# Elementwise work of the key stage moved from POOL to VectorE and ScalarE, and triangular inverses taken three batches at a time

## The chip, the cores and the metric

One NeuronCore of one Trainium2 chip. The metric is the device time of one execution in microseconds; lower is better. The engines are named as in the profile: PE (TensorE; PEld its weight loads), DVE (VectorE), ACT (ScalarE), POOL (GpSimd), SP (SyncE, whose queue issues most transfers). In the kernel's code they are T, V, S, G and SP.

## What is computed

Two layers on 512 tokens of width 1024 (with 256 context tokens ahead of them in layer 0): an RWKV-7 mixer with inner width 2048, 32 heads of 64 and two directions, then a Hyena mixer (a long convolution). All in fp32. The change lies in layer 0, whose heart is this recurrence, run forwards (z = 0) and backwards (z = 1):

```
def step(s, inp):
    r_t, w_t, k_t, v_t, a_t, b_t = inp
    sa = jnp.einsum('bhvk,bhk->bhv', s, a_t)
    s = s * w_t[:, :, None, :] + sa[..., None] * b_t[:, :, None, :] + v_t[..., None] * k_t[:, :, None, :]
    return s, jnp.einsum('bhvk,bhk->bhv', s, r_t)
```

with a = -kk, b = kk * a_gate, kk the normalised key, w the decay, and k scaled by the gate. Beside it stands a bonus, the sum over a head of r * (k_0 + k_1) * r_k, times v, where k_0 and k_1 are the keys of the two directions.

## The kernel before

**Tiling.** The inner width is 16 pairs p of two heads (128 partitions). The 768 positions are 12 chunks of 64. Inside a chunk the recurrence becomes matrix products: with e the running product of decays, the scaled vectors ar (from kk and r, times e) and bk (from kk * a and k, divided by e) give a strictly triangular 64x64 matrix L for each head, chunk and direction, and the chunk needs the inverse of (I - L). Each L is taken as two 32x32 diagonal blocks, inverted by elimination, and one off-diagonal block that is put in later.

**Stages.** (1) Norms, mixes and the product for v. (2) The key stage: products for k and r run on PE; `k_out`, `k_norm` (normalise), `decays` (decay and gate from small products, tanh, and a running sum along each chunk: the scan instruction), `key_side` (exponentials, bk, ar, gam) and `strict_side` (L by PE, stored to DRAM as ld; ar, bk, gam stored too) work through the 16 pairs and both directions; `bonus` follows each pair. (3) The scan stage: `merge` completes the inverses of a pair (its transfers are issued by POOL, MQ = G.dma_start), `fetch` and `prep` load and prepare chunks, and `chain` runs the recurrence for two pairs at a time, in 8 rounds of 12 steps; products for the gate (g), read-out and output product run beside it. (4) Filters and layer 1, untouched by the change. In the profiled execution the key stage's pairs run from about 300 to 775 us and the chain from 884 to 1697 us.

**The inverses** (`inverse`, lines 1228 to 1245). The 384 units of a direction (16 pairs x 2 heads x 12 chunks) are cut into 6 batches of 64. A batch is a tile lt of 128 partitions (64 units x 2 diagonal blocks) by 32x32, loaded from ld by two SP transfers. For j = 1 to 30 DVE multiplies a column by a row into ltm, j x (31-j) elements, and adds that to lt: 60 dependent instructions. POOL then clears the other triangle (affine_select) and sets the diagonal, and SP stores the batch to td. With two directions there are 12 batches; IB = 2 of a direction's 6 belong to the key stage, the others to the scan stage. A batch may start when both directions have stored enough pairs (`ready_inv`, line 1252); `merge` of a pair waits for its batches.

**Who runs what.** Tuples such as E_KE name the engines an operation may use (lines 1033 to 1038): E_CU scales the decay argument, E_TA the gate ta, E_KE and E_ET are the two products k * em and em * ta, E_AR and E_RC the two halves of ar. In `bonus` and for gam the engine is fixed.

**The order of the work** is not written out by hand. `run` (line 255) holds a set of lanes, each a generator that yields operations, and places one operation after another by a list schedule: of all next operations the one that the cost model (`Model.price`, line 183) lets start first. Where an operation may go to several engines, the price is added to the start and the smaller sum wins. The model prices DVE at 0.064 us + n/960 (n/1920 for one input in SBUF), ACT at 0.1 + n/1200 and more for tensor scale and bias. Each engine then executes its own list in order. The key stage ends when all its lanes (`key_lanes`, line 1257, the inverses of IB among them) are done, the products of g apart; only then the lanes of the scan stage are added.

**A step of the chain** (lines 1498 to 1551): products into PSUM, copied to xs by ACT and DVE; a product with the inverse, copied into sv by ACT and DVE; a product giving bs; DVE adds the carried state (sa = bs + sc); DVE multiplies sa by the decay gam into the next step's sv, one half of the partitions at a time; POOL forms the next sc = sa * gam. sa has one buffer, sc two.

## Time and profile before

| | us |
|---|---|
| median of 3 runs | 2401.1 (2401.01 to 2407.73) |
| the profiled execution | 2397.8 |
| its span, first to last instruction | 2396.1 |

| engine | busy us, share of the span |
|---|---|
| PE | 2054.1, 86% |
| PEld (weight loads, beside PE) | 1625.3, 68% |
| DVE | 1776.7, 74% |
| ACT | 1067.5, 45% |
| POOL | 650.5, 27% |

The time that counts is that of the whole execution; the span leaves out what lies before the first and after the last instruction. Busy time is the union of an engine's instructions. All instructions go through one helper line (58), so the profile is read by the names of tiles: `out<-in`. Shapes are partitions x elements.

### The profile page before, as it was taken

To read this page: it belongs to the slowest core of one execution; us is meant where nothing else is said; L and a number is where in the kernel's file an instruction comes from. 1 tells how busy PE (TensorE), PEld (TensorE's weight loads), DVE (VectorE), ACT (ScalarE), POOL (GpSimd) and SP (SyncE) were. 2 spreads that over 40 slices of the span, in tenths; PEclk is the share of its full clock that TensorE was granted. 3 is DMA by queue.
4 is the path that set the end of the run, shared out by engine and by line. 5 is a ranking of instruction groups with operands and counts; after the bars stand their busy time and mean duration, and the time that the engine had idled before them with its cause. 6 is when DMAs were issued, how large, how long until landed. Compare 5 with 4: busy or idle time off the path is not lost.

```text
span 2396.1 us, 53878 instructions
## 1 busy us (share of the span) xinstructions
PE 2054.1 (86%) x21710; PEld 1625.3 (68%) x21710; DVE 1776.7 (74%) x2971; ACT 1067.5 (45%) x1891; POOL 650.5 (27%) x745
## 2 busy tenths in 40 slices
PE   6699888779787688778888788898769999999997
PEld 2588666567665567666666667676447787878786
DVE  1955399999997677777888787767677675757666
ACT  2534576657664234333445344434444333333333
POOL 0400174655564422233233233321132100000000
PEclk8799999989988898888999999999989999999999
DMA  7155666747467675646585754554456523223232
GB/s 235 47 182 196 210 203 191 227 161 239 167 199 240 179 187 142 155 121 145 152 187 135 160 144 127 144 125 133 128 178 206 179 79 105 84 89 103 82 121 78
DMA packets 317568, 369.29 MB, mean 154 GB/s; under 512 B 132387, under 2 KB 203630, under 8 KB 317320
## 3 DMA queue, kind: packets, MB, share of 16 engines
q1 hardware_dynamic: 303832, 330.34, 47.0%
q0 software_dynamic: 13488, 35.52, 5.1%
q8 instruction: 171, 2.80, 0.5%
q14 instruction: 77, 0.63, 0.1%
HBM read 262.79 MB, written 102.17 MB: 152 GB/s over the span
## 4 chain that ended last, share of the span: by engine, by line
PE 38%; DVE 18%; DMA 8%; issue 5%; SPq 3%; ACT 2%; POOL 2%; DVEq 0%; ACTq 0%; POOLq 0%
PE ps L58 38%; DVE sv L58 3%; SPq L58 3%; DVE ltm L58 2%; DVE lt L58 2%; DVE wlo L58 2%; DVE ar L58 2%; DMA tt<-td 1%; DMA lt<-ld 1%; DMA ar<-ard 1%; DVE cvv L58 1%; DVE sa L58 1%; DMA ar<-zd 1%; POOL tt L58 1%; DVE xs L58 1%
## 5 line engine op out<-in xcount | busy, mean ns | idle before, releaser
L58 PE MATMUL ps<-m,whi 128*128 128x512 f32 (+1 forms) x1536 | 419.9, 375 | 45.2 <-DVE ro L58 15.8
L58 DVE TENSOR_TENSOR wlo<-wraw,whi 128x512 fp32r<-128x512 f32 x320 | 245.9, 770 | 209.0 <-ACT whi L58 206.0
L58 ACT ACTIVATE whi<-wraw 128x512 fp32r<-128x512 f32 x320 | 200.9, 628 | 411.8 <-PE ps L58 321.9
L58 PEld LDWEIGHTS ps<-m,whi 128*128 128x128 f32 x1536 | 263.3, 197 | 102.2 <-DVE ro L58 17.0
L58 PE MATMUL ps<-ar,bk 128*64 128x64 f32 (+2 forms) x4096 | 224.7, 249 | 53.4 <-DVE ar L58 40.7
L58 PE MATMUL ps<-m,wlo 128*128 128x512 f32 (+1 forms) x768 | 245.9, 371 | 0.0
L58 PEld LDWEIGHTS ps<-ar,bk 128*64 128x64 f32 (+1 forms) x4096 | 193.5, 147 | 75.7 <-issue 42.9
L58 PE MATMUL ps<-h1h,whi 128*128 128x512 f32 x512 | 201.1, 393 | 1.7 <-DVE cx L58 1.1
L58 PE MATMUL ps<-h1l,whi 128*128 128x512 f32 x512 | 199.9, 390 | 0.4 <-DVE h1l L58 0.4
L58 PE MATMUL ps<-h1h,wlo 128*128 128x512 f32 x512 | 199.8, 390 | 0.0
L58 POOL TENSOR_TENSOR sc<-sa,gam 128x256 f32<-128x256 f32 x80 | 66.4, 831 | 449.1 <-DVE sa L58 439.9
L58 DVE TENSOR_TENSOR ltm<-lt 128x30 f32<-128x30 f32 (+4 forms) x360 | 154.2, 428 | 25.2 <-DMA lt<-ld 13.6
L58 DVE TENSOR_TENSOR lt<-lt,ltm 128x30 f32<-128x30 f32 (+4 forms) x360 | 149.7, 416 | 9.6
L58 PEld LDWEIGHTS ps<-m,wlo 128*128 128x128 f32 x768 | 133.9, 197 | 25.9 <-issue 2.8
L58 POOL TENSOR_TENSOR res<-res,gt 128x512 f32<-128x512 f32 x4 | 5.4, 1372 | 498.6 <-ACT junk L58 498.6
L58 DVE TENSOR_TENSOR ar<-ps,cst 64x512 f32<-64x512 f32 (+1 forms) x192 | 115.0, 599 | 16.7 <-PE ps L58 11.3
L58 PE MATMUL ps<-sv,bt 128*64 128x64 f32 x1408 | 92.0, 242 | 26.2 <-DVE sv L58 13.8
L58 PEld LDWEIGHTS ps<-h1h,whi 128*128 128x128 f32 x512 | 96.2, 188 | 21.3 <-issue 1.5
L58 PEld LDWEIGHTS ps<-h1l,whi 128*128 128x128 f32 x512 | 96.2, 188 | 20.4 <-DVE h1l L58 1.5
L58 PEld LDWEIGHTS ps<-h1h,wlo 128*128 128x128 f32 x512 | 96.1, 188 | 19.6
L58 PE MATMUL ps<-sv,ar 128*64 128x64 f32 x1536 | 89.0, 238 | 20.9 <-DVE sv L58 19.2
L58 PEld LDWEIGHTS ps<-sv,bt 128*64 128x64 f32 x1408 | 70.1, 148 | 53.5 <-DVE sv L58 19.8
(292 smaller groups left out, 4739.9 us busy)
## 6 DMA issues: line engine op xcount, KB each, us to landing
wraw<-wg SPq DMA_DIRECT2D x128, 256.0 KB
wraw<-w SPq DMA_DIRECT2D x128, 256.0 KB
aw<-ada_w SPq DMA_DIRECT2D x96, 256.0 KB
bkd<-bk SPq DMA_DIRECT2D x32, 768.0 KB
ard<-ar SPq DMA_DIRECT2D x32, 640.0 KB
ar<-ard SPq DMA_DIRECT2D x128, 128.0 KB
ar<-zd SPq DMA_DIRECT2D x128, 128.0 KB
wraw<-w_out SPq DMA_DIRECT2D x64, 256.0 KB
```

Source lines behind the costliest of these rows:

```text
L58: return getattr(self.eng.eng, self.fn)(*self.a, **self.k)
```

## The change

- The tuples lose G: E_CU and E_TA become (S, V); E_KE, E_ET and E_RC become (V,); the two POOL operations of the bonus go to DVE and the copy of gam to ACT.
- `inverse` handles NI = 3 batches in one tile, [128, 3, 32, 32], with the same 60 instructions, each three times as long. Six loads come ahead, three stores behind. IB = 1 triple of a direction (of 2) belongs to the key stage, and `ready_inv` asks for three batches' worth of pairs, that is 192 units, 8 pairs.
- In the chain sa is no longer a tile: the sum is made in sc, and POOL multiplies sc in place. sc has one buffer.
- l21 in `merge` loses its direction axis (the directions lie in different partitions), and the space reserved for the descriptors of POOL's transfers is halved.

```diff
@@ -536,6 +536,7 @@
     ard = [[tl(dr, f"ard{p}_{z}", [P, NC + NCX, C]) for z in range(2)] for p in range(NP)]
     NU = NP * 2 * NC
     UB = 64
+    NI = 3
     NB = NU // UB
     ld = [tl(dr, f"ld{z}", [C, NU, C]) for z in range(2)]
     td = [[tl(dr, f"td{z}_{b}", [2, UB, 32, 32]) for b in range(NB)] for z in range(2)]
@@ -1030,12 +1031,12 @@
     AB = 1
     MB2 = 0.0
     KN = 1
-    E_CU = (S,G)
-    E_TA = (S,G)
-    E_KE = (G,V)
-    E_ET = (V,G)
+    E_CU = (S,V)
+    E_TA = (S,V)
+    E_KE = (V,)
+    E_ET = (V,)
     E_AR = (V,)
-    E_RC = (G,)
+    E_RC = (V,)
     lring, gamring, bkring = Ring(LB), Ring(2), Ring(BS)
     taring, curing, arring = ([Ring(n) for _ in range(2)] for n in (DT, DC, AB))
     ktile, pair, uses = {}, {}, {}
@@ -1147,7 +1148,7 @@
         bb, em = bk[:, :, 0], bk[:, :, 1]
         yield S.activation(out=em, in_=cu[:, :, tok], func=AF.Exp, scale=-1.0)
         yield S.activation(out=cu, in_=cu, func=AF.Exp)
-        yield G.tensor_copy(out=gam[:, :, z:z + 1], in_=cu[:, :, last:last + 1])
+        yield copy(S, gam[:, :, z:z + 1], cu[:, :, last:last + 1])
         while p not in ktile:
             yield
         k, nk = ktile[p]
@@ -1211,9 +1212,9 @@
             yield
         ts = [gset[p, z][0][:, NCC:] for z in range(2)]
         q = ts[0]
-        yield G.tensor_tensor(out=q, in0=q, in1=ts[1], op=ADD)
+        yield V.tensor_tensor(out=q, in0=q, in1=ts[1], op=ADD)
         used(p, ("ta", 1), 2, gset[p, 1][1])
-        yield G.tensor_tensor(out=q, in0=q, in1=k[:, NCC:], op=MUL)
+        yield V.tensor_tensor(out=q, in0=q, in1=k[:, NCC:], op=MUL)
         used(p, "k", 3, ktok[p])
         yield V.scalar_tensor_tensor(out=q, in0=q, scalar=pcol("r_k", p), in1=r, op0=MUL, op1=MUL)
         used(p, "r", 3, rt_)
@@ -1227,30 +1228,34 @@
 
     def inverse(z, bt):
 
-        lt = tl(sysp[0], "lt", [P, 32, 32], sysp[1])
-        u0 = bt * UB
-        for bl in range(2):
-            q = slice(32 * bl, 32 * bl + 32)
-            yield dma(out=lt[HR[bl]], in_=ld[z][q, u0:u0 + UB, q].rearrange("s u t -> u s t"))
-        v = lt[:, ::-1, ::-1] if z else lt
-        tmp = tl(sysp[0], "ltm", [P, 240], sysp[2])
+        lt = tl(sysp[0], "lt", [P, NI, 32, 32], sysp[1])
+        for k in range(NI):
+            u0 = (bt * NI + k) * UB
+            for bl in range(2):
+                q = slice(32 * bl, 32 * bl + 32)
+                yield dma(out=lt[HR[bl], k], in_=ld[z][q, u0:u0 + UB, q].rearrange("s u t -> u s t"))
+        v = lt[:, :, ::-1, ::-1] if z else lt
+        tmp = tl(sysp[0], "ltm", [P, NI * 240], sysp[2])
         for j in range(1, 31):
             w = 31 - j
-            tv = tmp[:, 0:j * w].rearrange("p (a b) -> p a b", b=w)
-            yield V.tensor_tensor(out=tv, in0=v[:, 0:j, j:j + 1].broadcast_to([P, j, w]), in1=v[:, j:j + 1, j + 1:32].broadcast_to([P, j, w]), op=MUL)
-            yield V.tensor_tensor(out=v[:, 0:j, j + 1:32], in0=v[:, 0:j, j + 1:32], in1=tv, op=ADD)
-        yield G.affine_select(out=lt, in_=lt, pattern=[[2 * z - 1, 32], [1 - 2 * z, 32]], compare_op=ALU.is_gt, fill=0.0, base=0, channel_multiplier=0)
-        yield G.memset(lt.rearrange("p a b -> p (a b)")[:, ::33], 1.0)
-        yield dma(out=td[z][bt].rearrange("b u s t -> (b u) s t"), in_=lt)
-        invdone.add((z, bt))
-
-    IB = 2
+            tv = tmp[:, 0:NI * j * w].rearrange("p (k a b) -> p k a b", k=NI, b=w)
+            yield V.tensor_tensor(out=tv, in0=v[:, :, 0:j, j:j + 1].broadcast_to([P, NI, j, w]),
+                                  in1=v[:, :, j:j + 1, j + 1:32].broadcast_to([P, NI, j, w]), op=MUL)
+            yield V.tensor_tensor(out=v[:, :, 0:j, j + 1:32], in0=v[:, :, 0:j, j + 1:32], in1=tv, op=ADD)
+        yield G.affine_select(out=lt, in_=lt, pattern=[[0, NI], [2 * z - 1, 32], [1 - 2 * z, 32]], compare_op=ALU.is_gt, fill=0.0, base=0,
+                              channel_multiplier=0)
+        yield G.memset(lt.rearrange("p k a b -> p k (a b)")[:, :, ::33], 1.0)
+        for k in range(NI):
+            yield dma(out=td[z][bt * NI + k].rearrange("b u s t -> (b u) s t"), in_=lt[:, k])
+            invdone.add((z, bt * NI + k))
+
+    IB = 1
     invdone = set()
     keys = [Lane([(decays, p, z) for p in range(NP)]) for z in range(2)]
     bons, norms = Lane(), Lane()
 
     def ready_inv(_, b):
-        return min(ldone) * 2 * NC >= (b + 1) * UB
+        return min(ldone) * 2 * NC >= (b + 1) * NI * UB
     invs = Lane([(inverse, z, b) for b in range(IB) for z in range(2)], 1, lambda z, b: ready_inv(z, b))
     mods1 = Lane([(adaln, ((0, 2), (1, 0), (1, 1), (1, 2)), adp, 128, 4, 1, (adp, "arow"))], 1, lambda *a: True, MB2)
     rlane2 = Lane([(rate_loads, p) for p in range(NP)])
@@ -1320,14 +1325,14 @@
     def merge(p):
 
         tt = tts[p % len(tts)]
-        l21 = rt("l21", [P, 2, NC, 32], LBUF)
+        l21 = rt("l21", [P, NC, 32], LBUF)
         t1 = rt("t1", [P, 2, NC, 32], 1)
         for z in range(2):
             f = slice(32 * z, 32 * z + 32)
             g = slice(32 - 32 * z, 64 - 32 * z)
             for h in range(2):
                 u = (p * 2 + h) * NC
-                yield MQ(out=l21[64 * h + 32 * z:64 * h + 32 * z + 32, z], in_=ld[z][f, u:u + NC, g])
+                yield MQ(out=l21[64 * h + 32 * z:64 * h + 32 * z + 32], in_=ld[z][f, u:u + NC, g])
                 for bl in range(2):
                     rr = slice(64 * h + 32 * bl, 64 * h + 32 * bl + 32)
                     cs = slice(32 * bl, 32 * bl + 32)
@@ -1346,7 +1351,7 @@
         for c in range(NC):
             for z in range(2):
                 for f, g in rows[z]:
-                    yield T.matmul(b[g, c, :], lhsT=l21[f, z, c, :], rhs=t1[f, z, c, :], start=True, stop=True)
+                    yield T.matmul(b[g, c, :], lhsT=l21[f, c, :], rhs=t1[f, z, c, :], start=True, stop=True)
         m1 = tl(rx, "m1", [P, NC, 32], 1, tag="t1")
         yield copy((S, V), m1, b)
         t[0] = True
@@ -1493,7 +1498,7 @@
         sv, stok = svs.pop(0)
         for h in range(2):
             yield G.memset(sv[h][HR[h]], 0.0)
-        sc = rt("sc", [P, 2, 2, C], 2)
+        sc = rt("sc", [P, 2, 2, C])
         yield G.memset(sc, 0.0)
         for n in range(NC):
             g, i = divmod(n, 4)
@@ -1528,17 +1533,15 @@
                 bs = quad("pn")
                 for q, z, h in QZH:
                     yield T.matmul(bs[HR[h], q, z, :], lhsT=BT[q][z][:, lc[z], HR[h]], rhs=sv[h][:, q, z, :], start=True, stop=True)
-                sa = rt("sa", [P, 2, 2, C])
-                yield V.tensor_tensor(out=sa, in0=bs, in1=sc, op=ADD)
+                yield V.tensor_tensor(out=sc, in0=bs, in1=sc, op=ADD)
                 while not svs:
                     yield
                 nsv, ntok = svs.pop(0)
                 gv = gf[:, :, two(2 * (base[0] + lc[0]), 2 * (base[1] + lc[1]) + 1)].unsqueeze(3).broadcast_to([P, 2, 2, C])
                 for h in range(2):
-                    yield V.tensor_tensor(out=nsv[h][HR[h]], in0=sa[HR[h]], in1=gv[HR[h]], op=MUL)
+                    yield V.tensor_tensor(out=nsv[h][HR[h]], in0=sc[HR[h]], in1=gv[HR[h]], op=MUL)
                 if n < NC - 2:
-                    sc = rt("sc", [P, 2, 2, C], 2)
-                    yield G.tensor_tensor(out=sc, in0=sa, in1=gv, op=MUL)
+                    yield G.tensor_tensor(out=sc, in0=sc, in1=gv, op=MUL)
             if g:
                 for q, z, h in QZH:
                     yield T.matmul(by[HR[h], q, z, :], lhsT=sv[h][:, q, z, :], rhs=ARB[q][:, h, z, lc[z], :], start=False, stop=q + z == 2)
@@ -1663,7 +1666,7 @@
     W_PREP = 2
     W_YS = 1
     ys, reads = Lane(width=W_YS, bias=B_YS), Lane([(filter_base,)], bias=B_READ)
-    invs = Lane([(inverse, z, b) for b in range(IB, NB) for z in range(2)], 1, lambda *a: True, B_INV)
+    invs = Lane([(inverse, z, b) for b in range(IB, NB // NI) for z in range(2)], 1, lambda *a: True, B_INV)
 
     def ready_merge(p):
         return zeroed and all((z, b) in invdone for z in range(2) for b in range(-(-(p + 1) * 2 * NC // UB))) \
@@ -2071,7 +2074,7 @@
     import concourse.bacc as _bacc
     from concourse.bass_utils import run_bass_kernel_spmd as _run
 
-    nc = _bacc.Bacc("TRN2", target_bir_lowering=False, num_devices=1, dynamic_dma_scratch_size=8192)
+    nc = _bacc.Bacc("TRN2", target_bir_lowering=False, num_devices=1, dynamic_dma_scratch_size=4096)
     arrays = layout(inputs)
     I = {n: nc.dram_tensor(n, v.shape, mybir.dt.from_np(v.dtype), kind="ExternalInput").ap() for n, v in arrays.items()}
     out = nc.dram_tensor("out", (TX, D), F32, kind="ExternalOutput").ap()
```

## Rows read from the trace of the kernel before

**Rows 1.** The four stages: busy us of each engine (instructions), TensorE clock, DMA share, GB/s
```profile
300.00:775.00 475.00, 387.15 (x3165) 297.65 (x3163) 443.63 (x522) 308.31 (x506) 284.12 (x217) 0.93 0.63 202
775.00:884.00 109.00, 79.94 (x964) 62.50 (x964) 67.28 (x160) 32.78 (x55) 40.82 (x65) 0.89 0.76 199
884.00:1425.00 541.00, 453.79 (x8781) 363.13 (x8782) 435.76 (x970) 220.02 (x457) 155.92 (x242) 0.91 0.60 146
1425.00:1697.00 272.00, 238.78 (x4523) 188.76 (x4520) 194.29 (x350) 117.47 (x232) 71.69 (x112) 0.96 0.50 129
```

**Rows 2.** Key stage, DVE: groups by shape | busy us, mean ns | idle before
```profile
L58 DVE TENSOR_TENSOR wlo<-wraw,whi 128x512 fp32r<-128x512 f32 x59 | 62.6, 1063 | 11.9 <-ACT whi L58 11.8
L58 DVE TENSOR_TENSOR_SCAN cu<-scanm,cu 128x780 f32<-128x780 f32 x28 | 56.2, 2009 | 0.0
L58 DVE TENSOR_TENSOR ar<-nk,cu 128x768 f32<-128x768 f32 x32 | 42.8, 1339 | 0.0
L58 DVE SCALAR_TENSOR_TENSOR bk<-nk,bk 128x768 f32<-128x768 f32 x30 | 33.5, 1119 | 2.5 <-ACT bk L58 2.5
...
L58 DVE TENSOR_TENSOR l2l<-l,l2h 128x512 fp32r<-128x512 f32 x13 | 13.7, 1050 | 0.0
```

**Rows 3.** The same work by tile, whole run: ns least/median/most, first and last start
```profile
L58 DVE TENSOR_TENSOR wlo<-wraw,whi x59: 659/692/2335, 312.0 to 774.1; 128x512 fp32r<-128x512 f32 x59
L58 DVE TENSOR_TENSOR_SCAN cu<-scanm,cu x32: 1751/1776/3445, 273.9 to 745.7; 128x780 f32<-128x780 f32 x32
L58 DVE TENSOR_TENSOR ar<-nk,cu x32: 930/953/2568, 301.2 to 760.4; 128x768 f32<-128x768 f32 x32
```

**Rows 4.** Key stage, POOL: groups | busy us, mean ns
```profile
L58 POOL TENSOR_TENSOR ar<-r,cu 128x512 f32<-128x512 f32 x32 | 49.2, 1539 | 0.1
L58 POOL TENSOR_TENSOR bk<-kk,bk 128x768 f32<-128x768 f32 x21 | 47.0, 2243 | 0.0
L58 POOL TENSOR_SCALAR ta<-ta,kah,ka 128x768 f32<-128x768 f32 x24 | 45.1, 1881 | 49.3 <-DVE bk L58 45.1 <-DMA wraw<-wg 3.0 <-DMA bod<-ta 1.2
L58 POOL TENSOR_SCALAR cu<-cu,cc 128x768 f32<-128x768 f32 x13 | 19.4, 1489 | 4.8 <-ACT cu L58 4.7
```

**Rows 5.** The triangular inverses: busy us (instructions) of DVE, ACT, POOL before and in the scan
```profile
300.00:775.00 475.00, 142.02 (x240) 0.00 (x0) 7.75 (x8) 0.93 0.63 202
775.00:1425.00 650.00, 161.82 (x480) 0.00 (x0) 11.64 (x16) 0.90 0.63 155
```

**Rows 6.** Scan stage, DVE: the inverses' largest and smallest shape | busy us, mean ns
```profile
L58 DVE TENSOR_TENSOR lt<-lt,ltm 128x240 f32<-128x240 f32 x16 | 6.5, 406 | 0.4
L58 DVE TENSOR_TENSOR lt<-lt,ltm 128x30 f32<-128x30 f32 x16 | 3.1, 196 | 0.5
```

**Rows 7.** One-input work on DVE, tile nn: ns least/median/most
```profile
L58 DVE TENSOR_SCALAR nn<-hd x3: 411/418/419, 821.1 to 905.2; 64x512 f32<-64x512 f32 x3
```

**Rows 8.** SP's loads for the inverses by tile: ns least/median/most to issue one
```profile
L58 SPq DMA_DIRECT2D lt<-ld x24: 579/1354/3408, 366.3 to 1326.4; - x24
```

**Rows 9.** Scan stage, DVE: the chain's groups | busy us, mean ns
```profile
L58 DVE TENSOR_TENSOR sv<-sa,gam 64x256 f32<-64x256 f32 x110 | 61.9, 562 | 3.4
L58 DVE TENSOR_TENSOR sa<-ps,sc 128x256 f32<-128x256 f32 x55 | 23.3, 424 | 12.5 <-PE ps L58 10.5
```

**Rows 10.** One step of the chain, instructions in order of time: start us, us
```profile
1005.18 0.42 DVE L58 TENSOR_TENSOR sa<-ps,sc 128x256 f32<-128x256 f32 x1
1005.64 1.18 DVE L58 TENSOR_TENSOR sv<-sa,gam 64x256 f32<-64x256 f32 x2
1005.69 0.86 POOL L58 TENSOR_TENSOR sc<-sa,gam 128x256 f32<-128x256 f32 x1 [6.68 <-DVE sa L58]
```

**Rows 11.** The same multiplications by tile: ns least/median/most
```profile
L58 DVE TENSOR_TENSOR sv<-sa,gam x176: 405/420/858, 884.2 to 1697.7; 64x256 f32<-64x256 f32 x176
```

**Rows 12.** Waits in 884 to 1425 us: total us, times, longest
```profile
PE ps L58 <- DVE sv L58: 26.2, 43, 5.2
```

**Rows 13.** POOL's transfers for the merges by tile: ns least/median/most to issue one
```profile
L58 POOL DMA_DIRECT2D tt<-td x144: 560/615/694, 796.9 to 1558.9; - x144
```

## The prediction

> **What bounds the kernel now.** I read first the busy time of each engine by stage [rows 1]. In the key stage (300 to 775 us) DVE is busy 443.6 of 475 us, 93.4%, and PE 387.2, 81.5%: DVE sets the pace and PE idles 88 us behind it. In the scan stage no engine is full. While inverses run beside the chain (884 to 1425) PE is busy 84% and DVE 81%; afterwards (1425 to 1697) PE 88% and DVE 71%, with the granted clock up from 0.91 to 0.96. So the change is worth what it takes from DVE in the first stage, and what PE waits for DVE in the second.
>
> Then I read the key stage's DVE groups [rows 2] against the medians of the same instructions [rows 3]. The mean is far above the median everywhere: 1063 against 692 ns, 2009 against 1776, 1339 against 953. The same shape sometimes takes over twice its normal time, and POOL, busy 284 us [rows 1], works on the same tiles meanwhile [rows 4]. I take the excess as the price of the two running together.
>
> **The change, key stage.** *Excess returned.* Mean less median times count: wlo 59 x 0.371 = 21.9 us; cu 28 x 0.233 = 6.5; ar 32 x 0.386 = 12.4. Seven further groups, the first and last of which stand in the rows [rows 2], lose 37.2 the same way (0.953 us taken for 768 elements, 0.692 for 512). Together 78.0 us.
>
> *Inverses.* Before, 240 instructions (four batches) take 142.0 us here, while 480 (eight batches) take 161.8 later [rows 5]: 592 against 337 ns each. One instruction handles 165 elements on average (the sum of j(31-j) over 30). Between 30 and 240 elements the time goes from 196 to 406 ns [rows 6], 1.00 ns an element and 166 ns fixed. Three batches in one, 496 elements, give 0.66 us by that line; the nearest row, 512 elements at 692 ns [rows 3], gives 0.675, which I take. A triple is 60 x 0.675 = 40.5 us against 3 x 60 x 0.337 = 60.7. Two triples in this stage: 81.0 instead of 142.0, with six batches done instead of four. The Trainium skill (Perfetto Trace Analysis, Optimizing Scalar/DVE Operations) puts the overhead of a DVE instruction on SBUF at about 60 ns. By it the 480 instructions that go away would save only 29 us; by the 166 ns of the rows it is 80, and the measurement decides.
>
> *Work returned to DVE.* The 42 products on bk (21 of them in [rows 4], 21 more of the same shape) at 0.953: 40.0 us. The 32 products ar<-r,cu and 32 of the bonus at 0.692: 44.3. POOL's 24 + 13 scalings of ta and cu [rows 4] now choose between ACT and DVE. DVE's one-input work took 418 ns for 512 elements [rows 7], so 0.55 to 0.63 for 768. None on DVE gives 0, all 60 of the stage 38; the planner prices DVE at half of ACT, so I take 40 of them, 22 us. The small copies of gam go to ACT: 30, at most at ACT's mean of 0.61 us (308.3 / 506 [rows 1]), 18 us on an engine busy 65%, so nothing; without that cover each would hold up the bk products behind it.
>
> DVE in the stage: 443.6 - 78.0 - 142.0 + 81.0 + 40.0 + 44.3 + 22.0 = 411 us (389 to 427 by the ends). At the same 93.4% that is 440 us, a **gain of 35**, if the load is even. It is not: a triple needs the first eight of the sixteen pairs, so the inverses fall into the second half. First half: DVE 165, PE 387.2 / 2 = 193.6, which now bounds: 207 us at 93.4%. Second half: DVE 246, so 263. Together 471, a gain of 4. If PE holds only the 88% of 1425 to 1697, the first half is 220 and the stage loses 8. I take **15**, between the even and the uneven case, for pairs can run ahead only a little (three k buffers), with -8 and 35 as ends.
>
> *Transfers and queues.* The loads and stores of the inverses are as many as before (24 and 12), but six loads now go to SP in a row: 6 x 1.35 us [rows 8], 8 us in which weight loads stand behind them, four times. Two weight buffers are loaded ahead, so I count nothing; uncovered it is 32 us over the whole run. POOL's clearing of the other triangle becomes three times longer, about 6 us a triple (7.75 / 4 x 3, [rows 5]), but nothing waits for it until a merge. The transition (775 to 884) I leave alone.
>
> **The change, scan stage.** It is 96 steps in eight rounds; 55 of the sums stand in the first stretch [rows 9], 11 a round, so it holds 60 steps and the second 36. PE idle per step is (541 - 453.8) / 60 = 1.45 us against (272 - 238.8) / 36 = 0.92. The excess, 0.53 x 60 = 32 us, goes with the inverses; their DVE time falls from 161.8 to 81, so half of it goes: **16** (0 to 32).
>
> The step: POOL starts sc right after sa, beside the two sv products [rows 10], and these take 1.18 us together where two medians make 0.84 [rows 11]; the mean of 562 ns [rows 9] says that it is so in most steps. In place, sc has to wait until both products have read it. The chain gains 0.34 us in 80 steps, 27 us; PE's wait for sv is 26.2 in the first stretch [rows 12], but that counts both kinds of sv. I take **12** (0 to 26). The new wait holds POOL about 0.8 us longer, with copies of sv and merge transfers queued behind it; POOL had stood idle for 6.68 us before [rows 10], and the next sum needs sc a step later. What is late next is ACT's half of the copies and PE itself.
>
> Clock: at 0.96 instead of 0.91, 453.8 us would be 24 less; with half of the waits gone I take **10** (0 to 24).
>
> Sum: 15 + 16 + 12 + 10 = **53 us**. The profiled execution took 2397.8 (span 2396.1), so 2344.8; the median of the runs is 3.3 higher, so 2348.
>
> The smaller l21 and the dropped copy of sa cost nothing. The halved descriptor space is the slower rival's.
>
> **Rivals.** *Late inverses.* The two triples form one dependent line of 120 instructions, 81 us. If they lose against the key work they run at the stage's end: PE-bound pairs 387 / 0.934 = 414, plus 81, is 495, a loss of 20, against the scan's 38: 2383. For it: readiness comes only at the middle, and DVE is then 94% asked for. Against: before, batches of the same priority ended at their time.
>
> *No difference.* PE takes over as the bound at 88% (the key stage loses 8) and the scan is held by PE's order, so that only one of its three terms comes: within 7 us of 2401.
>
> *The slower side: POOL's transfers.* The space for POOL's descriptors is halved. Now one transfer takes 615 ns to issue and never over 694 [rows 13], so nothing stalls. There are 144 of these and 64 more for l21, 13 a merge. If a full ring made each as long again, POOL would lose 8 us a merge, 128 in all; sc and the sv copies stand behind them. Above 53 / 16 = 3.3 us a merge that reaches the chain the change loses; at half the price and more, 64, it gives 2412. Against: POOL is idle 71% of the scan, and merges run ahead.
>
> *DVE stays saturated.* If the excess is not POOL's doing, 106 us come back to the engine that bounds the stage. The point is 53 x 0.934 = 50 us of the 139 lost (78 and, for the inverses, 142.0 - 240 x 0.337 = 61) staying; with 100 staying it is 2348 + 107 = 2455. The Trainium skill (same page and section) says that work may well be moved off a saturated DVE, even to GpSimd, but adds that the two share a port, so that moving between them might not help; by its first half the change would lose. The trace bears out the second half, for DVE's products grow most while POOL runs beside them [rows 10].
>
> **Chances.** Forecast 0.60; late inverses 0.19; no difference 0.08; POOL's transfers 0.08; DVE saturated 0.05. About 0.3% (7 us) is what a measurement of this kernel can tell from no change. Faster 0.79, same 0.08, slower 0.13. The ends of the terms reach from -8 to 117 us of gain; 2300 to 2402 holds the forecast but for its best corner (0.04), the late inverses and most of no difference, and leaves out the slower cases. The likeliest case alone: 2305 to 2375.
>
> **What would show it.** Right: wlo near 0.70 and ar near 0.95 us in the key stage; 240 inverse instructions in all, of 0.66 to 0.69 us; DVE near 410 us there; the two sv products 0.84 us together; idle of PE per step near 1.2 in the first rounds. Wrong: means that stay above 0.85 for wlo, inverses that end after the last pair's ld, POOL transfers above 0.7 us, or PE busy under 85% in a shorter key stage.

## The result, and the profile after

The changed kernel takes **2301.66 us** (median of 4 runs, 2296.43 to 2309.6) against 2402.41 (2401.01 to 2407.73): a ratio of 0.958, interval 0.9548 to 0.9611, 100.7 us faster. The forecast was 2348, the range 2300 to 2402. The profiled execution of after took 2309.6 us (span 2307.7), the slowest of its four, so the two profiles are 88.2 us apart, not 100.7.

The stages of the changed kernel, which answer to [rows 1], are the key stage, the transition, the first five rounds of the chain and the last three. Each line has the stretch, then the busy us of PE, PEld, DVE, ACT and POOL (with instructions), the granted TensorE clock, the DMA share and GB/s:

```profile
300.00:735.00 435.00, 395.41 (x3257) 301.03 (x3257) 398.62 (x530) 327.71 (x559) 11.29 (x38) 0.95 0.74 232
735.00:860.00 125.00, 94.02 (x1039) 71.74 (x1039) 86.64 (x142) 36.20 (x62) 50.46 (x67) 0.88 0.83 196
860.00:1347.00 487.00, 414.40 (x8710) 333.90 (x8706) 344.01 (x653) 196.67 (x403) 156.72 (x260) 0.93 0.63 152
1347.00:1601.00 254.00, 230.01 (x4454) 183.88 (x4452) 186.86 (x350) 110.96 (x217) 67.01 (x114) 0.97 0.49 130
```

POOL fell from 284.12 to 11.29 us in the key stage and the stage is 40 us shorter, with as much PE work in it. Three dates, counted from the span's start, divide the gain: the last store of ld, the chain's first sum and its last. The first two lines are before, the other two after:

```profile
L58 SPq DMA_DIRECT2D ld<-cu x64: 445/486/1527, 306.0 to 772.7; - x64
L58 DVE TENSOR_TENSOR sa<-ps,sc x88: 403/425/427, 883.8 to 1696.8; 128x256 f32<-128x256 f32 x88
L58 SPq DMA_DIRECT2D ld<-cu x64: 451/487/1530, 311.3 to 731.2; - x64
L58 DVE TENSOR_TENSOR sc<-ps,sc x88: 406/424/427, 859.7 to 1600.6; 128x256 f32<-128x256 f32 x88
```

Up to the last ld it is -41.5, in the transition +17.4 (128.5 instead of 111.1), in the chain -72.1 (740.9 instead of 813.0), and behind it +7.8 (707.1 instead of 699.3): together -88.4 of the span. Three later runs have the changed kernel's plan unaltered (the last three rows of the table below). Their chains take 738.0 to 740.8 us, but their last ld comes at 720.2 to 728.2, so the key stage's gain is 41 to 53 us, and the profile shown here has the least of it.

The groups of DVE in the key stage, beside [rows 2] and [rows 3] (busy us, mean ns | idle before):

```profile
L58 DVE TENSOR_TENSOR_SCAN cu<-scanm,cu 128x780 f32<-128x780 f32 x28 | 49.4, 1773 | 0.7 <-issue 0.7
L58 DVE TENSOR_TENSOR wlo<-wraw,whi 128x512 fp32r<-128x512 f32 x63 | 43.1, 684 | 13.9 <-ACT whi L58 13.1 <-PE ps L58 0.6
...
L58 DVE TENSOR_TENSOR ar<-nk,cu 128x768 f32<-128x768 f32 x32 | 30.4, 949 | 0.5 <-DMA ard<-ar 0.4
...
L58 DVE TENSOR_SCALAR ta<-ta,kah,ka 128x768 f32<-128x768 f32 x15 | 10.1, 674 | 0.1
...
L58 DVE TENSOR_SCALAR cu<-cu,cc 128x768 f32<-128x768 f32 x9 | 5.6, 617 | 3.6 <-ACT cu L58 3.4
```

These three means are now just below what the medians were [rows 3]: 684 ns where the mean was 1063, 949 for 1339, 1773 for 2009. Their whole excess is gone.

The inverses follow: busy us (instructions) of DVE, ACT and POOL in key stage, transition and scan, then by tile (ns least/median/most, first and last start). Their counterpart is [rows 5]:

```profile
300.00:735.00 435.00, 76.83 (x111) 0.00 (x0) 3.74 (x2) 0.95 0.74 232
735.00:860.00 125.00, 44.57 (x70) 0.00 (x0) 8.18 (x4) 0.88 0.83 196
860.00:1601.00 741.00, 41.87 (x60) 0.00 (x0) 3.73 (x2) 0.94 0.58 144
```

```profile
L58 SPq DMA_DIRECT2D lt<-ld x24: 585/1685/4632, 485.4 to 865.1; - x24
L58 POOL TENSOR_SCALAR_AFFINE_SELECT lt<-lt x4: 3462/3624/3840, 613.2 to 974.7; 128x3072 f32<-128x3072 f32 x4
```

All 12 batches take 163.3 us (303.8 before). POOL's clearing, which ends a triple's work, starts at 613.2 for the first and at 974.7 for the last of the four; the other two are at 739.9 and 840.0, so the second triple of the key stage ends 9 us behind the last ld.

Two steps of the chain's own work, beside [rows 10] and [rows 11]:

```profile
1007.01 0.42 DVE L58 TENSOR_TENSOR sc<-ps,sc 128x256 f32<-128x256 f32 x1 [0.76 <-PE ps L58]
1007.47 0.87 DVE L58 TENSOR_TENSOR sv<-sc,gam 64x256 f32<-64x256 f32 x2
...
1008.49 0.62 POOL L58 TENSOR_TENSOR sc<-sc,gam 128x256 f32<-128x256 f32 x1 [5.00 <-DVE sv L58]
```

The two sv products take 0.87 us together, where they took 1.18, and POOL's product starts when they are done and takes 0.62 instead of 0.86. What PE waits for sv over the whole chain (total us, times, longest), before and after, in answer to [rows 12]:

```profile
PE ps L58 <- DVE sv L58: 33.1, 61, 5.2
PE ps L58 <- DVE sv L58: 9.3, 20, 1.0
```

### The profile page after: what moved, and what is told of

It is laid out like the page before. It is cut to its first block, busy times and chain, and to the rows that moved or that the text cites. A ratio compares the mean times of both kernels' runs of the same rounds, so it can differ in the third digit from the quotient of the medians.

```text
span 2307.7 us, 53374 instructions
## 1 busy us (share of the span) xinstructions
PE 2032.2 (88%) x21710; PEld 1606.1 (70%) x21710; DVE 1650.6 (72%) x2646; ACT 1058.7 (46%) x1881; POOL 375.8 (16%) x583
## 4 chain that ended last, share of the span: by engine, by line
PE 52%; DVE 19%; DMA 12%; issue 5%; ACT 3%; SPq 2%; POOL 1%; DVEq 0%; ACTq 0%; POOLq 0%
PE ps L58 52%; SPq L58 2%; DVE wlo L58 2%; DVE bk L58 2%; DVE ar L58 2%; DMA aw<-ada_w 2%; DMA ar<-zd 2%; DMA wraw<-wg 2%; DVE ltm L58 1%; DVE ta L58 1%; DVE sv L58 1%; DVE lt L58 1%; DMA ar<-ard 1%; DVE cvv L58 1%; DMA tt<-td 1%
## 5 line engine op out<-in xcount | busy, mean ns | idle before, releaser
L58 DVE TENSOR_TENSOR wlo<-wraw,whi 128x512 fp32r<-128x512 f32 x320 | 225.8, 707 | 200.8 <-ACT whi L58 198.6
L58 PEld LDWEIGHTS ps<-ar,bk 128*64 128x64 f32 (+1 forms) x4096 | 186.7, 141 | 54.4 <-issue 22.0
L58 POOL TENSOR_TENSOR sc<-sc,gam 128x256 f32<-128x256 f32 x80 | 55.5, 694 | 421.6 <-DVE sv L58 413.5
L58 DVE TENSOR_TENSOR ltm<-lt 128x90 f32<-128x90 f32 (+14 forms) x120 | 81.1, 676 | 20.8 <-DMA lt<-ld 17.5
L58 PE MATMUL ps<-xs,tt 128*64 128x64 f32 x1536 | 68.5, 233 | 28.6 <-DVE xs L58 26.7
L58 POOL DMA_DIRECT2D tt<-td x144 | 87.1, 609 | 9.9 <-DMA zd<-tt 4.9
```

What stands on the lines that cost most here:

```text
L58: return getattr(self.eng.eng, self.fn)(*self.a, **self.k)
```

## The experiments

Every ratio is to the kernel before on the same chip. The dates and the chain's length come from the two rows shown above, of each kernel; g is the PE time that products of g take inside the chain, overlaps counted once.

| kernel | last ld | chain starts | chain, us | g, us | ratio |
|---|---|---|---|---|---|
| before | 772.7 | 883.8 | 813.0 | 24.0 | 1 |
| only POOL emptied | 761.5 | 875.8 | 781.0 | 10.8 | 0.9921 |
| only the sum in place | 775.2 | 885.0 | 780.1 | 24.3 | 0.9876 |
| both, single batches | 762.0 | 876.5 | 761.8 | 10.8 | 0.9816 |
| triples, POOL at work | 788.1 | 913.1 | 751.6 | 5.7 | 0.9919 |
| changed | 731.2 | 859.7 | 740.9 | 0 | 0.958 |
| half of the single batches early | 766.4 | 911.4 | 781.1 | 0 | 1.0037 |
| the same, later | 726.4 | 917.3 | 741.7 | 0 | 0.9851 |
| second triples soft | 721.6 | 847.0 | 776.0 | 0 | 0.9691 |
| second triples held | 728.3 | 844.4 | 778.3 | 0 | 0.9762 |
| no POOL beside the chain | 732.0 | 852.3 | 766.9 | 5.7 | 0.9708 |
| changed, smaller ring still | 728.2 | 857.7 | 740.8 | 0 | 0.9622 |
| changed, g held back | 720.2 | 847.1 | 738.0 | 0 | 0.9583 |
| changed, bias of 0.06 | 724.7 | 850.4 | 738.0 | 0 | 0.962 |

### One part at a time

**Only POOL emptied**: the kernel before with the engines of the key stage changed, and nothing else.

```diff
-    E_CU = (S,G)
+    E_CU = (S,V)
...
-    E_RC = (G,)
+    E_RC = (V,)
...
-        yield G.tensor_tensor(out=q, in0=q, in1=ts[1], op=ADD)
+        yield V.tensor_tensor(out=q, in0=q, in1=ts[1], op=ADD)
```

> The kernel before with only the key stage's elementwise work taken from POOL. If POOL caused the excess: means of wlo and ar at 0.69 and 0.95, inverse instructions at 0.34 instead of 0.59 us, DVE in the stage near 405 us instead of 444, the stage 35 to 45 us shorter, median 2355 to 2370. If the triples brought the key stage's gain: within 10 us of 2402, or slower, as 100 us come to a saturated DVE.

Measured: 2376.43 us, ratio 0.9921 (0.9886 to 0.9955), 19 us faster. Its key stage and its inverses there:

```profile
300.00:766.00 466.00, 401.50 (x3320) 305.90 (x3318) 398.86 (x660) 331.74 (x565) 13.97 (x44) 0.93 0.68 219
```

```profile
300.00:766.00 466.00, 79.11 (x240) 0.00 (x0) 6.69 (x8) 0.93 0.68 219
```

DVE has taken over most of POOL's work (the copies of gam and some of the scalings go to ACT) and is busy 45 us less than before (443.6). The 240 single inverse instructions take 79.1 us (330 ns each) where they took 142.0 [rows 5]: their excess, too, was POOL's. The durations are as expected, but the time is not: the last ld comes only 11 us sooner, where a stage shorter by 35 to 45 was expected. With DVE and PE each busy 86% of it, neither fills the stage. The chain is 32 us shorter, and 13 of that come back behind it (711.9 us instead of 699.3).

**Only the sum in place**: the kernel before without sa.

```diff
-                sa = rt("sa", [P, 2, 2, C])
-                yield V.tensor_tensor(out=sa, in0=bs, in1=sc, op=ADD)
+                yield V.tensor_tensor(out=sc, in0=bs, in1=sc, op=ADD)
...
-                    yield G.tensor_tensor(out=sc, in0=sa, in1=gv, op=MUL)
+                    yield G.tensor_tensor(out=sc, in0=sc, in1=gv, op=MUL)
```

> The kernel before with only the sum of the chain made in sc and multiplied there by POOL. If the step of the chain sets the pace: the two sv products at 0.84 instead of 1.18 us, 0.34 us a step in 80 steps, median 2375 to 2392. If PE's order sets it: products shorter all the same, median within 7 us of 2402.

Measured: 2368.3 us, 0.9876 (0.9832 to 0.9919), 27 us faster, 7 better than expected. All of it lies in the chain, which is 33 us shorter; 8 come back behind it (707.6 us), as in the changed kernel.

**Both, single batches**: the changed kernel with one batch to a tile.

```diff
-    NI = 3
+    NI = 1
...
-    IB = 1
+    IB = 2
```

> The changed kernel with inverses one batch at a time and two of six batches of a direction in the key stage, as before; all else as changed. If the inverses' DVE time counts, the scan stage gets eight batches of 20.2 us (162) instead of six at 13.5 (81): 16 to 32 us more in the first rounds, the key stage unchanged (81 us of inverses either way), median 2318 to 2335. If only POOL's absence counts, 2295 to 2310.

Measured: 2350.17 us, 0.9816 (0.9776 to 0.9856), 45 us faster: the sum of the two above (19 and 27), and slower than either expected range. What remains to the changed kernel, whose four measurements give 0.958 to 0.9622, is 46 to 57 us. It belongs to the triples, their later start and the two more batches of the key stage together.

**Triples, POOL at work**: the changed kernel with the key stage's work back on POOL.

```diff
-    E_CU = (S,V)
+    E_CU = (S,G)
...
-    E_RC = (V,)
+    E_RC = (G,)
...
-        yield V.tensor_tensor(out=q, in0=q, in1=ts[1], op=ADD)
+        yield G.tensor_tensor(out=q, in0=q, in1=ts[1], op=ADD)
```

> The changed kernel with the key stage's elementwise work back on POOL (engine tuples, bonus, copy of gam as before); triples, sum in sc and the rest stay. If the excess on DVE is POOL's doing, the means of wlo and ar in the key stage rise from 0.68 and 0.95 to about 1.05 and 1.3 us, DVE there does some 100 us less own work but pays 80 to 130 us of excess, the stage grows by 20 to 40 us, and the median is 2320 to 2345. If the excess has another cause, the means stay, DVE is freed of 100 us in a stage that it bounds, and the median falls to 2260 or below.

Measured: 2376.64 us, 0.9919 (0.9891 to 0.9948). Its key stage, its inverses in it, and wlo:

```profile
300.00:792.00 492.00, 408.58 (x3237) 311.70 (x3236) 444.82 (x425) 309.11 (x505) 293.63 (x203) 0.92 0.66 207
```

```profile
300.00:792.00 492.00, 112.37 (x120) 0.00 (x0) 8.80 (x4) 0.92 0.66 207
```

```profile
L58 DVE TENSOR_TENSOR wlo<-wraw,whi 128x512 fp32r<-128x512 f32 x64 | 65.6, 1029 | 15.0 <-ACT whi L58 14.9
```

The excess is back (1029 ns), and a triple's instruction takes 936 ns (112.37 / 120) against 692 (76.83 / 111). The last ld is 57 us later than in the changed kernel, and the time lies 32 us above the expected range. Against only the sum in place the triples have won nothing: it is 8 us slower, and the two intervals overlap. **The triples are worth some 50 us with POOL quiet and nothing with POOL at work**; the quiet POOL is worth 19 us without them.

### When the inverses run

**Half of the single batches early, and the same later.** Both have single batches and six of twelve in the key stage, as the changed kernel has in triples. In the first a batch starts as soon as its pairs are stored (after 3, 6 and 8 pairs); the second keeps all of them until 8 pairs are.

```diff
-    NI = 3
+    NI = 1
...
-    IB = 1
+    IB = 3
...
-        return min(ldone) * 2 * NC >= (b + 1) * NI * UB
+        return min(ldone) * 2 * NC >= 3 * UB
```

(The last two lines are in the second alone.)

> The changed kernel with inverses one batch at a time, three of six batches of a direction in the key stage, each ready as soon as its pairs are stored (3, 6 and 8). Against the run with late single batches it differs in timing alone. If timing counts, PE drops to some 38 of 50 us from 400 us on and the ratio is 0.01 or more above that run's. If grouping counts alone, both ratios agree within 0.004.

> The changed kernel with inverses one batch at a time, three of six batches of a direction in the key stage, and none of them ready before eight pairs are stored: the same six batches at the same time as the triples, in 360 instructions instead of 120. If it is the timing that lets PE run freely in the first half, PE is busy 48 of 50 us until about 500 us as with the triples, and the ratio to before is 0.955 to 0.968. If it is the grouping, the second half pays 121 us of inverses instead of 81 and more gaps: chain start 25 to 50 us later than with the triples, ratio 0.973 to 0.99.

Measured: 2403.82 us, 1.0037 (1.0017 to 1.0057), for the first; 2358.74, 0.9851 (0.9827 to 0.9874), for the second. The 50 us from 400 on, the first kernel, the second, and the changed one:

```profile
400.00:450.00 50.00, 39.00 (x307) 29.84 (x306) 43.66 (x80) 33.26 (x57) 1.71 (x5) 0.86 0.57 179
```

```profile
400.00:450.00 50.00, 48.50 (x414) 36.82 (x412) 49.52 (x66) 42.07 (x72) 0.48 (x4) 1.00 0.71 239
```

```profile
400.00:450.00 50.00, 48.54 (x414) 36.82 (x412) 49.51 (x66) 42.03 (x72) 0.49 (x4) 1.00 0.73 238
```

Without inverses in the way PE is busy 97% at the full clock (granted 1.00, the upper of its two levels, 2.4 GHz); with early ones it is 39 us of 50 at 0.86, though DVE is not full. The kernel with only POOL emptied, whose single batches start early too, shows the same in these 50 us: 38.78 at 0.86. The later start lets the pairs end 40 us sooner, so **with POOL quiet it is the late start, and not the grouping, that shortens the key stage**. But 360 single instructions then don't fit behind the key work. From the last ld to the chain the second kernel shows:

```profile
730.00:917.00 187.00, 132.36 (x1228) 95.86 (x1228) 132.19 (x357) 38.63 (x74) 35.29 (x53) 0.75 0.59 152
```

90.4 us of the 132.2 are inverses, and the clock falls to 0.75. This is the rival of late inverses, and the triples, a third as many dependent instructions, are what keeps it away. The first kernel's expectation on timing holds: its ratio is 0.022 above that of both, single batches (0.9816). Of the second kernel's two expectations each holds in one half: PE is busy as timing alone would have it, and the ratio is that of grouping, with the chain 58 us later instead of 25 to 50. Why early batches hold the pairs up by so much, the runs do not settle: PE's waits there end with ar on DVE (23.7 us between 350 and 740), but the second kernel, with DVE fuller, has 5.0 us of them.

**Second triples held, and soft.** Pairs 8 to 15 need the second two triples only in round 4. The first kernel holds them until four pairs are merged; in the second they only give way (a larger bias in the planner).

```diff
-    invs = Lane([(inverse, z, b) for b in range(IB, NB // NI) for z in range(2)], 1, lambda *a: True, B_INV)
+    invs = Lane([(inverse, z, b) for b in range(IB, NB // NI) for z in range(2)], 1, lambda *a: len(mrgd) >= 4, B_INV)
```

```diff
-    B_INV = 0.05
+    B_INV = 1.0
```

> The changed kernel with the second two triples held back until four pairs are merged, since only rounds 4 to 7 need them. Theory: the chain's start at 860 is bound by the work on the way to the first merges, and the 44.6 us that DVE spends on the second triples from 735 to 860 stand in its way; without them the chain starts 5 to 20 us earlier, and in the scan the triples cost about 5 us a pair of them, so 0 to 15 us faster than the changed kernel. Rival: the first triples themselves (the second of them ends at 740) and the merge transfers set the start, so it stays within 4 us of 860, and the scan gets longer by 5 to 10 us.

> The changed kernel with the planner's bias for the second two triples at 1.0 us instead of 0.05, so that they give way to other work but are not held back. Between the changed kernel (chain 860 to 1601, 45 us of the second triples on DVE ahead of the chain and 42 in the scan) and the kernel with them held until four merges (chain 844 to 1623, 86 us of inverses in the scan, 37 us longer chain). Theory: an instruction of 0.7 us in the scan stands in the way of the chain's short ones on DVE, so what counts is how much of the inverses lies in the scan: the chain gets about 0.85 us longer for each us of inverse more in the scan, and starts at most 16 us earlier; with 10 to 30 us moved it comes out 0 to 15 us slower than the changed kernel. Rival: it was the hold itself that cost, since the merges of pairs 8 and on came late (one gap of 34 us between two steps); then the softer bias keeps the earlier start without the late merges, and it is 5 to 15 us faster.

Measured: 2339.47 us, 0.9762 (0.9739 to 0.9785), held; 2322.7, 0.9691 (0.9661 to 0.9721), soft. The chain starts 13 to 15 us sooner than in the profile of the changed kernel, but the last three rows of the table, with that kernel's plan, start it at 847.1 to 857.7. So the date alone shows nothing. From the last ld to the chain the changed plan takes 125.7 to 129.5 us, soft 125.4 and held 116.1: holding the triples back brings 10 to 13 us there, and the softer bias none. The chain is 35 to 37 us longer in both, against a scatter of 3 in the changed plan. The loss lies in its first four rounds: 427.3 us (soft) and 433.4 (held) from the first sum to that of the fifth round, against 391.6. It does not go by the inverses that moved: 13 us of them with soft, 44 with held (55.0 and 86.0 us in the chain against 41.9). Neither theory holds as put: soft has a late gap of 41.1 us between two sums at 1233, where the transfers of the next merges are only being issued, but also gaps of 33 and 28 us earlier, and the changed kernel's longest is 22.6.

### The other suspects

**A smaller ring still.** The changed kernel with half of the descriptor space again.

```diff
-dynamic_dma_scratch_size=4096
+dynamic_dma_scratch_size=2048
```

> The changed kernel with the space for POOL's descriptors halved once more, 2048 for 4096. If a full ring holds POOL back, issues of the merge transfers grow from 0.61 to 0.9 us and more, and the ratio is above 0.965. If the ring never fills, 0.61 us and 0.955 to 0.961 as in the changed kernel.

Measured: 2303.06 us, 0.9622 (0.9599 to 0.9645), the changed kernel's time. Its transfers for the merges come first, then those of the changed kernel:

```profile
L58 POOL DMA_DIRECT2D tt<-td x144: 562/617/654, 765.2 to 1463.4; - x144
```

```profile
L58 POOL DMA_DIRECT2D tt<-td x144: 560/615/652, 768.6 to 1466.2; - x144
```

No issue is longer than it was before [rows 13]: the slower rival's price is nil here.

**No POOL beside the chain**: an attempt to beat the changed kernel by taking the rest of POOL's elementwise work outside the chain as well.

```diff
-    E_SB = (V, G)
+    E_SB = (V,)
...
-    E_FL = (G,V)
+    E_FL = (V,)
...
-    E_GT = (G,V)
+    E_GT = (V,)
...
-    E_FH = (G,)
+    E_FH = (V,)
```

> The changed kernel with the other elementwise work that POOL shares with DVE also given to DVE: shifts in the first stage, the low parts of the filters, the two products with the residual gates (layer 0's rows and the last rows). Excess on DVE beside them should go (the rows' product of 1024 elements at 1.1 instead of up to 5.1 us, the last rows 1 to 3 us earlier): ratio 0.950 to 0.957. If DVE has no room there or the excess is not POOL's: 0.958 or more.

Measured: 2323.86 us, 0.9708 (0.9685 to 0.9731): slower than the changed kernel by 20 us or more. It gains some at the ends (the key stage's first ld comes at 299.2 against 305.9 to 312.6 in the four profiles of the changed plan, what follows the chain is 3.5 us shorter), and the chain, whose code is untouched, gets 26 us longer; 5.7 of them are g's. What the other 20 are, the runs do not show.

**Products of g held back, and a bias of 0.06.** One was to bring the four last g products back into the chain, the other to see what a change of plan without a change of work does.

```diff
+                while g == 3 and p >= 12 and not scanning:
+                    yield
                 while bring.full():
...
+    scanning = []
...
+    scanning.append(1)
```

```diff
-    B_INV = 0.05
+    B_INV = 0.06
```

> The changed kernel with the last 4 of the 16 g products held back until the scan stage begins, as many as the kernel before has there (96 matmuls, 33.7 us of PE). Theory: in the changed kernel PE has idle time at the end of the key stage and in the transition (94.0 busy of 125 us) that these products fill, so holding them back moves neither the last ld (731) nor the chain's start (860) by over 10 us and makes the chain's 741 us longer by 25 to 35: about 2328, 20 to 35 slower than the changed kernel. Rival: PE is the bound of the key stage too, so that whatever is taken out there starts the chain as much earlier: chain at 826 to 835, chain length 770, total the same within 7 us.

> The changed kernel with nothing altered but the planner's bias for the scan stage's inverses, 0.06 us instead of 0.05, which stands for no work at all. Theory: a list schedule that takes another turn somewhere is worth up to 1% in either direction in this kernel, and this, not work, is the 26 us that the chain lost in the kernel without any elementwise work on POOL outside the chain; so here the total moves by 3 to 20 us either way with the same busy times. Rival: the order is robust, the time stays within 4 us of the changed kernel, and those 26 us have a cause in work that was moved.

Measured: 2296.43 us, 0.9583 (0.9564 to 0.9602), and 2301.95, 0.962 (0.9589 to 0.965). Both edits left every engine's instructions in the changed kernel's order, so neither expectation was tried: they are two more samples of the changed kernel, 5 us apart. The gate came too late, since in the changed kernel's plan the last g products stand behind the key stage anyway. (The 33.7 us of the first expectation counts overlapping matmuls twice; they take 24.0, as shown below.)

## Why the prediction was right, and where it was not

The direction held, and so did the cause on which most of it rests, that POOL's work lengthens DVE's. The size did not: 88 us between the profiles against 53. The time lies inside the range by 1.7 us and outside what the likeliest case alone was given, 2305 to 2375. That it lies inside is in part luck, for errors of both signs stand behind it: key stage +26 and chain +34 beyond the forecast, transition -17 and what follows the chain -8, neither of which was forecast. Term by term:

**The excess on DVE: right, and larger than counted.** Shown from both sides, by taking POOL's work away alone (1063 to 685 ns for wlo) and by giving it back (1029). The prediction told the inverses' 142 to 81 us as the work of triples; emptying POOL alone brought four single batches to 79. Of the 140.5 us that all 12 batches save on DVE (303.8 to 163.3), 61 come with both, single batches, which still takes 242.7, and 79 with the 480 instructions fewer of the triples, the 80 worked out from the rows. DVE was put at 411 us for the stage and was 398.6: 24 scalings, not 40, came to it, at 617 and 674 ns, above the 550 to 630 estimated. The Trainium skill (Perfetto Trace Analysis, Optimizing Scalar/DVE Operations) says that DVE and GpSimd share a port and that moving work between them might not help. Moving it to GpSimd had cost here: DVE does 45 us less since it took the work back.

**The key stage: 15 forecast, 41 at the last ld.** The step that failed is the uneven halves, which priced the late inverses as a loss of 31 us against an even load. It put the first half at 207 to 220 us and the second at 263. The first loads of inverses, at 485, divide them: 185 and 246 us.

```profile
300.00:485.00 185.00, 178.20 (x1566) 137.36 (x1566) 172.18 (x225) 155.25 (x266) 1.80 (x15) 1.00 0.71 234
485.00:731.00 246.00, 213.21 (x1675) 160.39 (x1674) 222.64 (x300) 171.85 (x291) 9.49 (x23) 0.92 0.75 229
```

PE's 193.6 us for the first half had been taken at the clock of a starved PE, 0.93 [rows 1]; fed, it runs at 1.00 and is busy 178.2 of the 185 us, 96%. So the first half did not eat the gain of the even case, and the stage came out at 435 us by the borders of [rows 1], 5 below that case's 440. The even case itself does not hold either. With only POOL emptied and the batches early, DVE's 398.9 us at 93.4% would make a stage of 427 us, and it took 466. The late start gains: single batches early or late put the last ld at 766.4 or 726.4.

One cost that was put at nothing left a mark. SP takes 11.6 and 12.6 us for the six loads of a triple, not 8, and ACT waits for weight loads 14.5 us in the stage (7.9 to 10.8 in the three runs with the same plan), where before it was 2.0. How much of this the six loads cause and what of it reaches the stage, no run separates: half of the single batches early, with two loads in a row, has 10.4.

```profile
629.36 12.61 SPq L58 DMA_DIRECT2D lt<-ld  x6
ACT whi L58 <- DMA wraw<-wg: 14.5, 5, 4.8
```

**The transition: 0 forecast, 17 lost.** The late inverses came in small, and with them the prediction's own sign of being wrong: the second triple ends behind the last ld, by 9 us. From the last ld to the first merge transfer it is 37 us (731.2 to 768.6) instead of 24. From there to the chain it is 4 more, with the second triples beside the merges. Holding these back shortens the whole transition by 12 against the profile shown.

**The chain: 38 forecast, 72 measured.** 813.0 us were 692.6 of PE's work and 120.4 of its idle time; 740.9 are 644.3 and 96.6. The idle time fell by 24, where sum in place and inverses were to bring 28, and per step in the first five rounds it is 1.21 us ((487 - 414.4) / 60), as forecast. PE's own work fell by 48, where the clock was to bring 10. **24.0 of these were not in the prediction at all**: 96 matmuls of g that stood in the chain before.

```profile
L58 PE MATMUL ps<-m,whi 128*128 128x512 f32 x64 | 21.0, 410 | 0.0
L58 PE MATMUL ps<-m,wlo 128*128 128x512 f32 x32 | 12.7, 398 | 0.0
```

```profile
883.80:920.00 36.20, 24.03 (x96) 0.96 0.46 124
```

This is the kernel before, first between the chain's first and last sum, then both groups together in its first 36 us (PE, clock, DMA share, GB/s). The two take turns on PE and their records overlap, so their times do not add up. After has none there. The last g product ends at 920 before and 859 after. A PE that waits less in the key stage and is done sooner takes them ahead of the chain: they go with the key stage in the table too (10.8 with POOL emptied, 5.7 and 0 with triples). That these matmuls cost the chain their full time is read from the two traces; the run that was to show it changed nothing.

The other 24 us are PE's remaining work, done faster. An estimate from the granted clock of the whole chain, 0.92 before and 0.94 after, is 14. The first products of a step, which take the carried sv, show a second part; the lines are before, only the sum in place, and after:

```profile
L58 PE MATMUL ps<-sv,ar 128*64 128x64 f32 x1504 | 87.4, 239 | 20.9 <-DVE sv L58 19.2
L58 PE MATMUL ps<-sv,ar 128*64 128x64 f32 x1504 | 78.2, 237 | 15.5 <-DVE sv L58 12.7 <-issue 1.5
L58 PE MATMUL ps<-sv,ar 128*64 128x64 f32 x1504 | 73.2, 234 | 4.1 <-DVE sv L58 2.9
```

One matmul takes nearly as long as before (239 and 234 ns), yet together they occupy 14 us less: more of them overlap. The two parts share some of their time, and no run parts them.

**Its two parts.** In place was put at 12 and measures more: 33 us of chain in the kernel before, 19 with POOL emptied, and 27 and 26 us of the whole time. The triples were put at 16 and bring 10 (761.8 - 10.8 against 740.9) for 91 us of inverses fewer in the chain. That single ones of 0.34 us find gaps would explain it; no run shows it. Both are less sure than they look, for two kernels with the same work in the chain, half of the batches early and later, differ by 39 us there. The in-place sum has one more witness: PE's wait for sv, 38.2 us with POOL emptied, is 15.5 when the sum is in place too. With POOL at work in the key stage it hardly moves in sum (33.1 and 31.9), but that counts both kinds of sv; for the carried one, in the lines above, it goes from 19.2 to 12.7.

**The rivals.** Late inverses: real with single batches, 90.4 us of them behind the last ld where 81 were named. No difference: no. POOL's transfers: not at half of the space, nor at a quarter. A saturated DVE: shown false.

## What to carry to other kernels

When an engine's mean duration stands far above its median, look for who runs beside it before optimising its instructions; the work may be cheaper on the busy engine than beside it. An engine that is busy 93% of a stage need not be its bound: here 45 us less on DVE alone brought the last ld 11 us sooner. Take a starved PE's busy time down by its clock before using it as a bound, and ask what later work a freed engine will pull forward: here that was about a quarter of the gain. Groups of matmuls that take turns must be counted together, or their overlap is counted twice. Two parts may need each other, so test each with and without the other. A date in one profile is worth what it is in several: the same plan started its chain anywhere from 847.1 to 859.7 us.

## What the runs showed that was not expected

- One-input work on 768 fp32 elements took 617 to 674 ns on DVE against 949 for two inputs: less of a saving than the 418 ns for 512 [rows 7] promised.
- POOL's product sc, which no longer runs beside the two sv products, went from 0.86 us in the step shown before to a median of 0.62 over 80 steps.
- The length of the chain scatters with the plan: 738 to 781 us in the kernels that do all of g ahead of it, with 42 to 86 us of inverses inside it, and not in the order of these. Within one plan it is 738.0 to 740.9.
